# The S5 step-difference kernels: small matmuls ordered by product instead of by group, and a skip diagonal on 128 rows

## The chip, the cores and the metric

The kernel runs on one NeuronCore of a Trainium2 chip. The metric is the device time of one launch in microseconds (us), from the first to the last instruction with the little that lies around them; lower is better.

## The reference

The reference computes two layers of a bidirectional encoder on 512 tokens of 1024 channels, in float32. Layer 0 mixes tokens with a convolution and with retention; layer 1 mixes them with a bidirectional S5 state-space layer, and a GLU follows. Every layer ends with an MLP of 4096 hidden units. Shifts, scales and gates of the norms come from a conditioning vector.

Of the S5 layer this matters here: 64 groups of 16 channels each drive, in two directions, a diagonal complex state of 64 numbers, and the output is a sum of both directions and a skip:

```
bu = einsum('sgc,gpc->sgp', u, f * b)          # complex, per direction
h  = scan(h = a * h + bu)                      # forward, and backward
y  = Re(C_f h_f) + Re(C_b h_b) + d_skip * u
```

The kernel works in chunks of 8 tokens. Within a chunk the output at step i depends on the input at step j through a 16x16 matrix that depends on i - j alone, one for each step difference from -7 to 7. These matrices ("the kernel of the steps within a chunk") are products of C, powers of a and B, and at step difference 0 both directions and the diagonal of `d_skip` add up. They depend on the parameters only.

## The kernel before

The work is one program. Its stages, in order of time, are the mixer of layer 0 (to about 245 us), the MLP of layer 0 (to about 696 us), the S5 layer with its GLU, and the MLP of layer 1.

The large products run on TensorE (PE) in `mm3` (called from `gemm`, line 226): each operand is split in two halves in a reduced float32 type, and three matmuls of 128x128 weights by 512 columns add up in PSUM. All of them go through `mm`, line 170. A weight unit of 1024x128 takes 24 such matmuls. Each unit is loaded on SP's queue (`load_unit`, line 177), copied to its upper half on ScalarE (ACT, line 197), and its lower half is formed on VectorE (DVE, line 192), up to four units ahead.

While the MLP of layer 0 runs, a background generator prepares the S5 matrices in DRAM: first `s5_powers` (line 886), then `s5_matrices` (line 1116). `step` (line 147) takes pieces of it as units of the MLP go by, counted in estimated VectorE time (`pace`, 3.6 us a unit at line 1666). The order within an engine is then settled by the framework's scheduler, which simulates the program, except where an instruction is pinned in program order; the background's transfers (`put`, line 1121, on POOL's queue) are pinned, its matmuls are not.

`s5_matrices` works through 8 batches of 8 groups, each in 2 halves `s` of 4 groups: 16 blocks. For each block VectorE (lines 862 and 870) makes `e` (128 rows = direction and state; per group 2 x 128 columns, the real and the imaginary part) and `wi`, and from each batch `bp` (per group 32 columns: 16 of one direction, 16 of the other, zeros elsewhere; its zeros are set on POOL, line 1187). POOL's queue loads `pb`, `bt`, `bc` and `dk`, and stores `d_e`, `d_wi` and `d_kr`. Then come the matmuls that this text is about (lines 1240 to 1252). They fill one PSUM tile `ps`; group n writes the 32 partitions from 32n, that is, column group n of the array:

- two products (r = 0, 1) of `bp[r]` (32 columns as weights) and `e` (128 columns), line 1244;
- two products of the second half of `bp[r]` (16 columns) and the 16 columns of `e` at step difference 0, line 1249;
- the skip, line 1251: a 16x16 identity and `dk`, the diagonals of `d_skip` on 16 rows.

The loop over the four groups is the outer one, so all five products of a group stand together. Everything is plain float32, for which each product shows as two MATMUL records in the trace. At the end ScalarE copies `ps` to `kk` (line 1254), and POOL's queue stores it; `windows` (line 1153) later spreads it into the matrices that the S5 layer loads.

Another place of the kernel already addresses the four column groups in turn: `vecmat` (line 353), which multiplies a vector by weights for the modulation. Its weights are a broadcast column of `cT` or `mod` on 32 columns, and its inner loop runs over the column groups.

Of the kernel before, what the change touches and what calls it, by code (L numbers as in the profile page):

```python
# [10 lines left out]
F32 = mybir.dt.float32  # L11
# [6 lines left out]
P = 128  # L18
# [9 lines left out]
EPS = 1e-6  # L28
# blocks of adaLN that VectorE works out
# [3 lines left out]
# ---------------------------------------------------------------- host layout  # L33
def _units(w):
    """(K, M) weights -> [M/128][K/1024][128 (k in tile)][8 (k tile)][128 (m)]."""
    k, m = w.shape
    v = w.reshape(k // 1024, 8, P, m // P, P)
    return np.ascontiguousarray(v.transpose(3, 0, 2, 1, 4)).reshape(m // P, k // 1024, P, 1024)


def _consts():
# [12 lines left out]
    # row (16 g + c): [(any step, c)], [g]  # L54
# [10 lines left out]
def _layout(i):  # L65
# [6 lines left out]
    # [layer][256 columns][half of k][k in tile][k tile][column]  # L72
    o["adn"] = f["ada_w"].reshape(2, 2, 4, P, 24, 256).transpose(0, 4, 1, 3, 2, 5).reshape(2, 24, 2, P, 1024)
    # the same with columns first: [blocks of ADT][half][column][k]
# [21 lines left out]
    # [(direction, state)][batch of 8 groups][c_re, c_im, b_re, b_im][group][channel]  # L96
# [3 lines left out]
    # [4 groups][(step, channel)][re, im][(group, direction, state)]  # L100
    bt = np.stack([f["s5_" + n][0].transpose(3, 1, 0, 2).reshape(16, 16, 512) for n in ("b_re", "b_im")], axis=2)
    o["bt"] = np.tile(bt.transpose(1, 0, 2, 3), (1, 8, 1, 1))
    # the skip's weights on the diagonals of [batch of 8 groups][channel][group][channel]
# [13 lines left out]
class Stream:  # L117
    """Weight units in order, loaded and split ahead of their use."""
# [17 lines left out]
class Kern:  # L136
# [9 lines left out]
    # ------------------------------------------------------------ helpers  # L146
    def step(self, us):
        """Run background pieces worth about `us` of VectorE time."""
        self.debt += us * self.rate
        while self.debt > 0 and self.bg:  # L150
            try:
                c = next(self.bg[0])
                self.debt -= c
            except StopIteration:
                self.bg.pop(0)
        if not self.bg:
            self.debt = 0.0
# [17 lines left out]
    def load(self, out, src):  # L175
        """A load on SP's queue, whose order is the program's."""
        self.tc.keep_in_program_order(self.nc.sync.dma_start(out, src))
# [25 lines left out]
    def mm3(self, ps, w, k, x, first, last):  # L203
        """ps += w[k].T @ x with both operands in exact halves."""
# [5 lines left out]
    def gemm(self, src, count, xs, done, group=1, pace=0.0, onto=(), last=True):  # L210
        """For the next units of the stream: done(m, psum of unit.T @ xs); the
        units of a group go side by side, with the K tiles outermost. `pace` is
        the background work per unit; the first units add to what is in `onto`;
        without `last` the sums of the second half go on later."""
# [17 lines left out]
    def split(self, src, dst=None, tag=("hh", "hl")):  # L232
        """Exact halves of a float32 tile in SBUF."""
# [7 lines left out]
    # ------------------------------------------------------------ statistics  # L241
    def col_sums(self, ps, col, tiles):
        """ps[t, col + b] = sum over channels (partitions and tiles) of token b * 128 + t."""
# [5 lines left out]
    def rsqrt(self, ps, n, scale, two=False):  # L249
        """(scale * ps[:, :n] + EPS) ** -0.5; with `two`, ps[:, n:2n] counts as well."""  # L250
# [15 lines left out]
    def bcast(self, ps, v):  # L266
        """ps[:, token] = v (tokens on partitions, [128, 4])."""
# [3 lines left out]
    def add_sq(self, i, t, last=False):  # L271
        """Collect the sum of squares over the channel tiles."""
# [13 lines left out]
    def stats(self, early=lambda: None):  # L286
        """The tokens' 1 / rms, tokens on partitions; `early` is called when TensorE
        only waits for the last square."""
        # has the square root's table loaded early
# [7 lines left out]
    def rstd(self, *between):  # L297
        """The tokens' 1 / rms, on all partitions. `between`: functions to be called before
        each of TensorE's two steps, and after them; what ada_fill has loaded goes along."""
# [15 lines left out]
    def ada_ends(self):  # L315
        """Ends what the last rstd has taken along."""
        for d in self.ends:
            self.ada_end(*d)

    def norm_tiles(self, tiles, pb, gs, sh):  # L320
        """Halves of x * gs / rms + sh for these tiles; VectorE starts a tile before it
        ends the one before."""
# [19 lines left out]
    # ------------------------------------------------------------ adaLN  # L342
# [3 lines left out]
    def ada_mm(self, blk):  # L346
        """blk: layer, 256 columns and their weights, on TensorE with the K tiles in
        four column groups of the array."""
# [4 lines left out]
    def vecmat(self, v, w):  # L353
        """v.T @ 256 columns; w: for each part of them, its weights of K tile k."""
# [12 lines left out]
    def vecmat_end(self, ps, row):  # L367
        """Its 256 columns to partitions."""
# [25 lines left out]
    def ada_bg(self, l, ns):  # L394
        """Generator: loads a block, takes it in hand a step later."""
# [18 lines left out]
    def silu_c(self, tiles):  # L414
        """silu(c) on all partitions, for ada_dve"""
# [8 lines left out]
    def ada_dve(self, l, ns, raws=()):  # L424
        """Generator: these blocks, of ADT, on VectorE."""
# [16 lines left out]
    def ada_fill(self, l, n):  # L442
        """Two blocks, loaded now, for the next rstd to put between its steps."""
        self.fill = [(l, n + i, self.ada_load(l, n + i)) for i in range(2)]

    def ada_half(self, l, n):
        """A block's weights where the halves of hidden states were."""
# [11 lines left out]
    # ------------------------------------------------------------ layer 0 mixer  # L459
    def mixer0(self):  # L460
        nc, tc, a = self.nc, self.tc, self.a
        with ExitStack() as st:
# [9 lines left out]
            with tc.tile_pool(name="first", bufs=1) as first:  # L472
                # of each pair of channel tiles the shift on TensorE, the scale on VectorE
# [112 lines left out]
            # v, tokens on partitions  # L586
# [27 lines left out]
            # retention, with the gate's projection in between  # L614
# [33 lines left out]
            # conv LayerNorm, SiLU  # L648
# [41 lines left out]
            # the first units of the output's projection, as far as the convolution's part goes  # L690
# [53 lines left out]
    # ------------------------------------------------------------ MLP  # L744
    def pre(self, l, i):
        """Halves of x * g * (1 + scale), for the units that go ahead of the statistics."""
# [10 lines left out]
    def mlp(self, l, pace=0.0, each=lambda n: None):  # L757
        nc, a = self.nc, self.a
        # of the outputs, half stay in PSUM over the next quarter of the hidden units
# [7 lines left out]
        # the first units: rstd * (W.T @ xg) + W.T @ shift  # L767
# [77 lines left out]
    # ------------------------------------------------------------ S5: matrices  # L845
    def ops(self):
        """VectorE operations that add up their time, and a function that takes it."""
# [38 lines left out]
    def s5_powers(self, w1, w2, fr, fi, wo):  # L886
        """Generator: the powers of the S5 states. Like every background piece
        it yields its VectorE time."""
# [12 lines left out]
        with tc.tile_pool(name="pa", bufs=1, reuse_waits="tile") as pa:  # L901
# [14 lines left out]
            def exp(o, x):  # L916
                """o = exp(x); t1..t4 are scratch."""
# [13 lines left out]
                # 2^k as the product of two powers  # L931
# [18 lines left out]
            # ph modulo 2 pi, in two rounds; the parts of 2 pi have few bits  # L950
# [34 lines left out]
            # powers of a: pw[m] = a^m, m = 0..8  # L985
# [18 lines left out]
            # f = (a - 1) / lam  # L1004
# [16 lines left out]
            # unit phasors of 8 theta, kept at length one  # L1021
# [21 lines left out]
            # f' = f * conj(E)  # L1043
# [3 lines left out]
            # the angle of the other direction has the other sign  # L1047
# [20 lines left out]
            # per direction: powers for the inputs (8 - j | j + 1) and the outputs (i | 7 - i)  # L1068
# [16 lines left out]
            def turns():  # L1085
                for r in range(2):
# [7 lines left out]
                    # row = (16 groups, 8 steps) of part b -> [step][group][state]  # L1094
# [4 lines left out]
            # tables cos/sin(theta k), 8 groups a time  # L1099
# [16 lines left out]
    def s5_matrices(self, pl):  # L1116
        """Generator: the S5 matrices of every group, left in DRAM."""
# [14 lines left out]
        with tc.tile_pool(name="pb", bufs=1, reuse_waits="tile") as pb_:  # L1132
# [3 lines left out]
            def load(h):  # L1136
                """The operands of the inputs' matrices of 4 groups."""
# [8 lines left out]

            def load_bc(b):
                bc = tl("bc", [4, B, 16])
                dk = pb_.tile([16, B, 16], F32, name="dk", tag="dk", bufs=2)
                put(bc.rearrange("p r g c -> p r (g c)"), a["bc"][b])  # L1150
                put(dk.rearrange("p g c -> p (g c)"), a["dsk"][b])
                return bc, dk
            def windows(q):
                """The kernel of the steps within a chunk of 16 groups: moves for later."""
# [4 lines left out]
                def join():  # L1159
                    # [c'][group][step difference + 7][c]  # L1160
# [3 lines left out]
                def row(j):  # L1164
                    # row (j, c') holds the window that starts at step difference -j
# [11 lines left out]
            for b in range(G // B):  # L1177
# [3 lines left out]
                # f * b with the directions in separate columns  # L1181
# [12 lines left out]
                # their place is free now  # L1194
# [6 lines left out]
                for s in range(2):  # L1201
# [10 lines left out]
                    # three products: wr (cr + ci), ci (wr + wi), cr (wi - wr)  # L1212
# [27 lines left out]
                    for n in range(4):  # L1240
                        o = ps[32 * n:32 * n + 32, 0:P]
                        at = dict(tile_position=(0, 32 * n))
                        for r in range(2):
                            nc.tensor.matmul(o, lhsT=bp[r][:, s * 4 + n, :], rhs=e[:, n, r, :], start=r == 0,  # L1244
                                             stop=False, **at)
                        # step difference 0: both directions and the skip
                        o = ps[32 * n:32 * n + 16, 0:16]
                        for r in range(2):
                            nc.tensor.matmul(o, lhsT=bp[r][:, s * 4 + n, 16:32], rhs=e[:, n, r, 112:128], start=False,  # L1249
                                             stop=False, **at)  # L1250
                        nc.tensor.matmul(o, lhsT=self.ident[0:16, 0:16], rhs=dk[:, s * 4 + n, :], start=False,  # L1251
                                         stop=True, **at)
# [9 lines left out]
    # ------------------------------------------------------------ S5: the mixer  # L1262
# [435 lines left out]
```

## Time and profile before

| what | value |
|---|---|
| runs (3) | 1253.43, 1257.18, 1257.36 us |
| median | 1257.18 us |
| span of the profiled execution | 1255.3 us |
| PE busy | 1214.7 us (97% of the span) |
| VectorE busy | 875.9 us (70%) |
| ScalarE busy | 476.4 us (38%) |
| POOL busy | 109.0 us (9%) |

The profiled execution is given by its span, from the first to the last instruction; it lies 1.9 us below the median of the runs and within their spread. Engines are named PE (TensorE's matmuls), PEld (its weight loads, which overlap the matmuls), DVE (VectorE), ACT (ScalarE), POOL (GpSimd) and SP. A matmul's recorded duration is its way through the array; the next one can start long before it ends, so the pace of a row of matmuls is read from their starts. "x4" says that four like instructions follow each other in one row. A row of the view by stretches gives the stretch and its length, then for PE, PEld, DVE, ACT and POOL the busy time with the number of instructions, then the granted PE clock as a share of full speed (1.00 is 2.4 GHz), the mean busy share of the 16 DMA engines and the GB/s that they moved. A row of waits gives the total, the number of times and the longest, in us.

### The profile page before, as it was taken

The numbers are of one execution on the slowest core, as the hardware profiler recorded it, in microseconds if no ns is written. First come the engines' busy times: TensorE is split into PE (matmuls) and PEld (weight loads), VectorE is DVE, ScalarE is ACT, GpSimd is POOL, SyncE is SP. The second block draws the span as 40 slices with busy tenths as digits, with TensorE's granted clock in tenths as the row PEclk, the third lists the DMA queues.
The fourth block names the chain that finished last, engine by engine and source line by source line (L and its number), as shares of the span: only waits on it lengthen the run. The fifth ranks groups of instructions, "written<-read, shape, count | busy, mean of one in ns | idle before, by whom it ended". The sixth has DMA issues, their size and how long they took to land.

```text
span 1255.3 us, 17711 instructions
## 1 busy us (share of the span) xinstructions
PE 1214.7 (97%) x6830; PEld 967.1 (77%) x6830; DVE 875.9 (70%) x1605; ACT 476.4 (38%) x752; POOL 109.0 (9%) x221
## 2 busy tenths in 40 slices
PE   6999999999999999999999898999999999999996
PEld 4777756787788788888877777788888888888885
DVE  6899995898989778787767899869743332332333
ACT  4424314435514313312422657343552432532530
POOL 0000000000021222234332100000000000000000
PEclk6999999999999999999999889999999999999998
DMA  9754340724446787778697867648433332332201
GB/s 353 253 185 159 124 168 32 230 92 185 144 160 233 229 253 254 247 252 246 174 320 221 341 248 286 223 144 276 168 101 101 101 101 85 101 101 85 83 1 67
DMA packets 65700, 223.59 MB, mean 178 GB/s; under 512 B 11168, under 2 KB 11552, under 8 KB 63568
## 3 DMA queue, kind: packets, MB, share of 16 engines
q1 hardware_dynamic: 48528, 174.63, 41.0%
q0 software_dynamic: 16512, 46.79, 12.3%
q8 instruction: 53, 0.87, 0.3%
q10 hardware_dynamic: 576, 1.05, 0.2%
q14 instruction: 31, 0.25, 0.1%
HBM read 197.77 MB, written 29.82 MB: 181 GB/s over the span
## 4 chain that ended last, share of the span: by engine, by line
PE 89%; DVE 7%; DMA 2%; issue 1%; ACT 1%; SPq 0%; DVEq 0%; ACTq 0%
PE ps L170 84%; PE ps L1244 3%; DVE wk L1289 2%; DMA raw<-adn 1%; DVE xt L1421 1%; DVE xt L1420 1%; PE ps L1251 1%; PE ps L1249 0%; DMA raw<-fc 0%; DMA x<-x 0%; DVE wk L1677 0%; DVE sr L1289 0%; DVE hx L1289 0%; ACT wh L197 0%; SPq L1642 0%
## 5 line engine op out<-in xcount | busy, mean ns | idle before, releaser
L197 ACT CAST wh<-raw 128x1024 fp32r<-128x1024 f32 x169 | 176.7, 1050 | 514.3 <-PE ps L170 453.2
L192 DVE TENSOR_TENSOR wl<-raw,wh 128x1024 fp32r<-128x1024 f32 x169 | 205.8, 1221 | 194.1 <-ACT wh L197 191.9
L170 PE MATMUL ps<-hh,wh 128*128 128x512 f32 x808 | 317.6, 399 | 4.2 <-ACT cm L789 1.8
L170 PE MATMUL ps<-hl,wh 128*128 128x512 f32 x808 | 317.2, 393 | 1.6 <-DVE hl L238 1.1
L170 PE MATMUL ps<-hh,wl 128*128 128x512 f32 x808 | 316.5, 392 | 0.8 <-DVE wl L192 0.8
L170 PE MATMUL ps<-fh,wh 128*128 128x512 f32 x544 | 216.5, 399 | 0.0
L170 PE MATMUL ps<-fl,wh 128*128 128x512 f32 x544 | 215.6, 397 | 0.0
L170 PE MATMUL ps<-fh,wl 128*128 128x512 f32 x544 | 215.3, 396 | 0.0
L170 PEld LDWEIGHTS ps<-hh,wh 128*128 128x128 f32 x808 | 152.4, 189 | 42.9 <-ACT wh L197 3.5
L170 PEld LDWEIGHTS ps<-hl,wh 128*128 128x128 f32 x808 | 152.8, 189 | 33.8 <-DVE hl L238 1.6
L170 PEld LDWEIGHTS ps<-hh,wl 128*128 128x128 f32 x808 | 152.7, 189 | 33.9 <-DVE wl L192 1.2
L170 PEld LDWEIGHTS ps<-fh,wh 128*128 128x128 f32 x544 | 102.4, 188 | 25.5 <-issue 1.2
L170 PEld LDWEIGHTS ps<-fh,wl 128*128 128x128 f32 x544 | 102.5, 188 | 24.6
L170 PEld LDWEIGHTS ps<-fl,wh 128*128 128x128 f32 x544 | 102.5, 188 | 24.1
L827 DVE SCALAR_TENSOR_TENSOR x<-ps,mod,x 128x512 f32<-128x512 f32 x40 | 30.0, 750 | 77.9 <-PE ps L170 77.8
L538 DVE SCALAR_TENSOR_TENSOR cacc<-apad,cvw,cacc 128x512 f32<-128x512 f32 x120 | 83.5, 741 | 0.0
L811 DVE TENSOR_TENSOR fl<-wk,fh 128x512 fp32r<-128x512 f32 x64 | 44.1, 689 | 21.5 <-ACT fh L810 21.5
L280 ACT ACTIVATE wk<-x 128x512 f32<-128x512 f32 x35 | 22.1, 631 | 52.5 <-DVE x L827 27.1
L862 DVE TENSOR_TENSOR w<-pb,bt 128x512 f32<-128x512 f32 x64 | 41.3, 686 | 0.6
L436 DVE SCALAR_TENSOR_TENSOR raw<-raw,x 128x512 f32<-128x512 f32 x52 | 33.2, 686 | 11.8 <-DMA raw<-adt 9.4
L807 ACT ACTIVATE wk<-wk 128x512 f32<-128x512 f32 x64 | 40.7, 635 | 1.5
L1244 PE MATMUL ps<-eb,bp 128*32 128x128 f32 x256 | 40.9, 279 | 0.0
(246 smaller groups left out, 1373.0 us busy)
## 6 DMA issues: line engine op xcount, KB each, us to landing
raw<-fc SPq DMA_DIRECT2D x128, 512.0 KB, 4.0
raw<-adn SPq DMA_DIRECT2D x50, 512.0 KB, 5.2
raw<-adt SPq DMA_DIRECT2D x34, 512.0 KB, 4.6
pb<-d_pw POOLq DMA_DIRECT2D x32, 256.0 KB, 8.0
bt<-bt POOLq DMA_DIRECT2D x16, 512.0 KB, 8.8
d_e<-eb POOLq DMA_DIRECT2D x16, 512.0 KB, 3.5
d_wi<-eb POOLq DMA_DIRECT2D x16, 512.0 KB, 7.3
wi<-d_wi SPq DMA_DIRECT2D x8, 1024.0 KB, 5.4
```

Of the source, the lines that this page charges most:

```text
L170: i = self.nc.tensor.matmul(out, lhsT=lhsT, rhs=rhs, start=start, stop=stop, **kw)
L192: self.keep(self.nc.vector.tensor_tensor(lo, raw, hi.bitcast(F32), SUB))
L197: self.keep(self.nc.scalar.copy(hi, raw))
L280: nc.scalar.activation(sq, t, AF.Square)
L436: self.keep(nc.vector.scalar_tensor_tensor(half, half, 1.0, self.cb[k], MUL, MUL, accum_out=v[:, 2 * k + h:2 * k + h + 1]))
L538: nc.vector.scalar_tensor_tensor(ac, ap[:, t:t + S], cvw[:, i * TAPS + t:i * TAPS + t + 1], ac, MUL, ADD)
L807: nc.scalar.activation(f, r, AF.Square)
L811: nc.vector.tensor_tensor(lo, f, hi.bitcast(F32), SUB)
L827: nc.vector.scalar_tensor_tensor(self.x[m], ps, gate[:, m:m + 1], self.x[m], MUL, ADD)
L862: V.tensor_tensor(o, x, y, op)
L1244: nc.tensor.matmul(o, lhsT=bp[r][:, s * 4 + n, :], rhs=e[:, n, r, :], start=r == 0, stop=False, **at)
L1289: pin(nc.vector.tensor_tensor(*args))
```

## The change

The loop over products becomes the outer one, and the loop over the four groups the inner one, in a small function `each`. The skip's operands get all 128 rows: the identity's first 16 columns are used on all its rows, and `dk` becomes two fixed tiles of 128 rows that POOL sets to zero once, of which the transfers fill rows 0 to 15. Comments are taken out elsewhere in the file, which shifts line numbers and no instructions.

```diff
+            dks = []
+            for n in range(2):
+                dk = pb_.tile([P, B, 16], F32, name=f"dk{n}")
+                nc.gpsimd.memset(dk, 0.0)
+                dks.append(dk)
+
             def load_bc(b):
                 bc = tl("bc", [4, B, 16])
-                dk = pb_.tile([16, B, 16], F32, name="dk", tag="dk", bufs=2)
+                dk = dks[b % 2]
                 put(bc.rearrange("p r g c -> p r (g c)"), a["bc"][b])
-                put(dk.rearrange("p g c -> p (g c)"), a["dsk"][b])
+                put(dk[0:16].rearrange("p g c -> p (g c)"), a["dsk"][b])
                 return bc, dk
...
                     ps = self.psum()
-                    for n in range(4):
-                        o = ps[32 * n:32 * n + 32, 0:P]
-                        at = dict(tile_position=(0, 32 * n))
-                        for r in range(2):
-                            nc.tensor.matmul(o, lhsT=bp[r][:, s * 4 + n, :], rhs=e[:, n, r, :], start=r == 0,
-                                             stop=False, **at)
-                        o = ps[32 * n:32 * n + 16, 0:16]
-                        for r in range(2):
-                            nc.tensor.matmul(o, lhsT=bp[r][:, s * 4 + n, 16:32], rhs=e[:, n, r, 112:128], start=False,
-                                             stop=False, **at)
-                        nc.tensor.matmul(o, lhsT=self.ident[0:16, 0:16], rhs=dk[:, s * 4 + n, :], start=False,
-                                         stop=True, **at)
+                    def each(rows, cols, ops, start=False, stop=False):
+                        for n in range(4):
+                            lhs, rhs = ops(n)
+                            nc.tensor.matmul(ps[32 * n:32 * n + rows, 0:cols], lhsT=lhs, rhs=rhs, start=start,
+                                             stop=stop, tile_position=(0, 32 * n))
+                    for r in range(2):
+                        each(32, P, lambda n: (bp[r][:, s * 4 + n, :], e[:, n, r, :]), start=r == 0)
+
+                    for r in range(2):
+                        each(16, 16, lambda n: (bp[r][:, s * 4 + n, 16:32], e[:, n, r, 112:128]))
+                    each(16, 16, lambda n: (self.ident[:, 0:16], dk[:, s * 4 + n, :]), stop=True)
```

## Rows read from the trace of the kernel before

**Rows 1.** The chain that ended last: its shares by line, and one piece.

```profile
PE ps L170 84%; PE ps L1244 3%; DVE wk L1289 2%; DMA raw<-adn 1%; DVE xt L1421 1%; DVE xt L1420 1%; PE ps L1251 1%; PE ps L1249 0%; DMA raw<-fc 0%; DMA x<-x 0%; DVE wk L1677 0%; DVE sr L1289 0%; DVE hx L1289 0%; ACT wh L197 0%; SPq L1642 0%
...
473.23 11.12 PE ps L170 x48
```

**Rows 2.** The view by stretches, over the 16 blocks.

```profile
430.00:690.00 260.00, 260.00 (x1528) 209.37 (x1527) 202.04 (x357) 73.26 (x108) 81.45 (x149) 1.00 0.79 244
```

**Rows 3.** PE's timeline around one block: start, length (us), instructions.

```profile
601.70 0.39 PE L170 MATMUL ps<-hh,wl 128*128 128x512 f32 x1
602.02 0.62 PE L1244 MATMUL ps<-eb,bp 128*32 128x128 f32 x4
602.48 0.26 PE L1249 MATMUL ps<-eb,bp 128*16 128x16 f32 x4
602.66 0.21 PE L1251 MATMUL ps<-dk,ident 16*16 16x16 f32 x2
...
605.16 0.50 PE L170 MATMUL ps<-hh,wh 128*128 128x512 f32 x1
605.49 0.39 PE L170 MATMUL ps<-hl,wh 128*128 128x512 f32 x1
```

**Rows 4.** The shapes: duration in ns (min, median, max), first and last start.

```profile
L1244 PE MATMUL ps<-eb,bp x256: 272/273/298, 434.9 to 687.5; 128*32 128x128 f32 x128
...
L1249 PE MATMUL ps<-eb,bp x256: 175/176/180, 437.3 to 687.7; 128*16 128x16 f32 x128
```

**Rows 5.** PE's timeline where a block is split in two.

```profile
630.22 0.39 PE L170 MATMUL ps<-hh,wl 128*128 128x512 f32 x1
630.54 0.41 PE L1244 MATMUL ps<-eb,bp 128*32 128x128 f32 x2
...
631.21 0.39 PE L170 MATMUL ps<-hl,wh 128*128 128x512 f32 x1
...
632.37 0.40 PE L170 MATMUL ps<-hh,wh 128*128 128x512 f32 x1
...
635.95 0.39 PE L170 MATMUL ps<-hh,wl 128*128 128x512 f32 x1
```

**Rows 6.** PE's timeline over one row of `vecmat`, then its first 0.09 us.

```profile
285.11 1.06 PE L170 MATMUL ps<-raw,mod 128*32 128x128 f32 x32
286.10 0.61 PE L170 MATMUL ps<-sel,adr 128*128 128x1 f32 x4
...
285.11 0.29 PE L170 MATMUL ps<-raw,mod 128*32 128x128 f32 x4
```

**Rows 7.** POOL: its memset; `pb`'s first load issued, and its first use.

```profile
L1187 POOL MEMSET bp<- x16: 307/312/389, 413.5 to 650.1; 128x256 f32 x16
...
410.70 1.26 POOL L1122 DMA_DIRECT2D pb<-d_pw  x2
...
432.96 1.28 DVE L862 TENSOR_TENSOR w<-pb,bt 128x512 f32<-128x512 f32 x2
```

**Rows 8.** The view by stretches: an earlier one, the first four blocks, one piece.

```profile
310.00:400.00 90.00, 90.00 (x421) 72.12 (x420) 80.50 (x187) 36.48 (x52) 10.75 (x20) 1.00 0.52 173
...
430.00:490.00 60.00, 60.00 (x361) 48.33 (x360) 48.29 (x91) 13.11 (x19) 16.89 (x32) 1.00 0.82 250
...
640.00:650.00 10.00, 10.00 (x68) 7.27 (x67) 5.62 (x8) 2.42 (x5) 1.15 (x3) 1.00 1.05 338
```

**Rows 9.** Who waited for whom, 430 to 690 us: total, times, longest.

```profile
DVE wl L192 <- ACT wh L197: 18.6, 16, 2.9
DVE raw L436 <- DMA raw<-adt: 7.9, 3, 2.8
DVE wk L1270 <- DMA wk<-k_chan: 5.9, 1, 5.9
DVE bp L862 <- POOL bp L1187: 4.6, 4, 1.3
PEld ps L1244 <- DVE w L862: 1.5, 4, 0.4
```

## The prediction

> **What bounds the kernel now.** I read three views in turn. The chain that ended last comes first: 84% of it is the large matmuls of line 170, and the three lines of the small matmuls, 1244, 1249 and 1251, stand in it too [rows 1]. Next, the view by stretches from 430 to 690 us, which holds all 16 blocks: PE is busy for 260.00 of 260.00 us at full clock, DVE for 202.04, POOL for 81.45, and the DMA engines for a share of 0.79 [rows 2]. So here, and this is the only place where the change acts, PE sets the time, and what PE is spared comes off the end as long as nothing else fills the gap. Last, PE's timeline shows what a block costs, by starts, since durations overlap.
>
> A large matmul takes 0.232 us (48 in 11.12 us [rows 1]). Around an unbroken block the large matmuls at 601.70 and 605.49 lie 3.79 us apart; two such steps would be 0.46, so the block costs 3.33 [rows 3]. Of this, 3.14 are four groups of 0.785 each (602.02 to 605.16), and 0.19 is the way in and out: the first small matmul starts 0.32 after the large one, not 0.23, and the second large one 0.33 after the first.
>
> Within a group, the four matmuls of 128 columns take 0.46 (602.02 to 602.48). The four of 16 columns last 0.176 each and 0.26 together, so their starts are (0.26 - 0.176) / 3 = 0.028 apart, and the skip starts 0.18 after the first of them: 0.10 of that is a pause. The next group starts 0.145 after the first of the two skip records (602.02 + 0.785 - 602.66), and one step of some 0.04 (0.21 together, less a length as of line 1249) between the two leaves again 0.10 as a pause [rows 3, 4]. The skip is the one product on 16 rows, and PE pauses before and after it.
>
> In 4 of the 16 blocks the scheduler has put the first product apart, with large matmuls between: 630.22 to 631.21 is 0.99, less 0.46 makes 0.53, and 632.37 to 635.95 is 3.58, less 0.46 makes 3.12; together 3.65 [rows 5]. One block is in four parts; with 0.32 for each further part (3.65 - 3.33) I put it at 3.33 + 3 x 0.32 = 4.3. All blocks: 11 x 3.33 + 4 x 3.65 + 4.3 = **55.5 us**.
>
> **The change, part by part.**
>
> *Products in turn over the column groups.* The nearest row is `vecmat`, which has the same shape (128 rows, 32 columns of weights, 128 moving columns, float32) and already goes over the four groups: 32 matmuls, eight rounds of four, take 0.99 us up to the next instruction (285.11 to 286.10). The first four alone end 0.29 after the first start, and one of this shape lasts 0.273 [rows 4], so they start within 0.02 of each other [rows 6]. Even with the last one's way out counted in, a round takes no more than 0.99 / 8 = 0.124, about what one matmul takes in its group now (0.46 / 4 = 0.115). The 16 matmuls of 128 columns in a block are four rounds of 0.115: 0.46 in place of 1.84.
>
> *The 16-column products and the skip.* The skip gets the row count, the columns and the shape of line 1249, so I price it as that. A block has 16 + 8 = 24 such matmuls in six rounds. No row shows this shape in turn over groups, so I bound it. Low: a round takes what one matmul takes in one group, 0.028, as it did for 128 columns; 6 x 0.028 = 0.17. High: each record needs 0.028 whatever its group, 24 x 0.028 = 0.67. I take the low end, since the burst of rows 6 has four starts within 0.02, under one such step; both ends stay for the range. The Trainium skill speaks for the high end: "TensorEngine Tiling (Array Packing)", section Instruction Overhead, says that each matmul carries an overhead of about 60 cycles and warns against tiling a dimension that is already small. By that rule 24 records of 25 ns (an estimate from that page: 60 cycles at 2.4 GHz) would take 0.60, and the burst in rows 6 disagrees with it only over four records.
>
> *The two pauses per group go*, eight of 0.10 in a block, since all products now have 128 rows; one exit of 0.10 stays at the block's end.
>
> A block then costs 0.19 + 0.46 + 0.17 + 0.10 = **0.92** (high end 1.42). If the same five blocks are split once, five times 0.32 is added. All blocks: 16 x 0.92 + 1.6 = 16.3, so PE is spared 55.5 - 16.3 = **39.2 us** (high end: 16 x 1.42 + 1.6 = 24.3, spared 31.2).
>
> *POOL.* Two memsets of 128x128 come ahead of the first loads; one of 128x256 takes 0.31 [rows 7], so at most 0.62 in all. `pb` is issued at 410.70 and first used at 432.96, so 22 us cover it: nothing. Without that cover the first block would be 0.62 later. The transfers into `dk` keep their number, bytes and place in POOL's queue. The fixed pair is reused every second batch, as the two buffers before: nothing. The weights of the skip have the columns of line 1249's. ScalarE's copy to `kk`, and POOL's memset of `bp` behind it, are only released earlier.
>
> *What is late next.* DVE keeps its 202.04 us, and the stretch shrinks to 260 - 39.2 = 220.8: DVE would be 91% busy. From 310 to 400 us it is 80.50 / 90 = 89% busy beside a PE without a gap [rows 8], so this is near what the kernel already bears. The waits of DVE for neither PE nor the casts (which themselves wait for PE) are 7.9 + 5.9 + 4.6 = 18.4 [rows 9]; 202.0 + 18.4 = 220.4 just fits into 220.8. In the first 60 us, with four blocks, it doesn't: 48.29 [rows 8] and their part of the waits by time, 18.4 x 60 / 260 = 4.2, are 52.5, where PE would need 60 - 4 x 2.45 = 50.2 (39.2 / 16 = 2.45). That is 2.3 us over, and PE's own waits for DVE at a block's start, 1.5 now [rows 9], will grow. I allow 3 us given back in all, between 0 and the 18.6 that DVE waits for casts [rows 9] if those waits should stay. The DMA share rises from 0.79 to 0.79 x 260 / 221 = 0.93; pieces at 1.05 run beside a full PE now [rows 8], so I cost it at nothing, with rival C if that fails.
>
> **Sum.** 39.2 - 3 = 36.2 us less. The working is in the time of one execution, whose span of 1255.3 us lies 1.9 under the median of the runs, within their spread; taken off the median, 1257.2 - 36.2 = **1221.0 us**.
>
> **The rivals.**
> A. *Forecast*, 1221.
> B. *Small records do not overlap*, the high end above: spared 31.2, and with DVE less pressed some 1 given back: 1227. For it: nothing shows a lasting pace under 0.028 a record. Against: the burst.
> C. *DVE or the transfers become the bound.* If DVE's 18.6 us of waits for casts stay beside the rest, the stretch cannot go below 220.4 + 18.6 = 239: spared 21, 1236. For it: DVE's stretches at 91%, and a DMA share of 0.93. Against: those casts wait for PE to free buffers, and PE will free them sooner; and rows 8.
> D. *The products do not overlap, only the pauses go* (the scheduler, which is free to order these matmuls, might also undo the turn): a block keeps 16 x 0.115 + 24 x 0.028 = 2.51 of its 3.14, so 0.63 x 16 = 10 us spared, 1247. Against: rows 6, the same shape in turn.
> E. *Slower: a change of column group pauses PE as a change to 16 rows does.* A block has 39 changes; at 0.10 each that is 3.9 on top of 2.51, 6.4 in place of 3.14, 16 x 3.3 = 52 us more, 1309. It decides from (3.14 - 2.51) / 39 = 0.016 us a change. Against: rows 6 change the group at every matmul, and 32 of them take 0.99 in all.
>
> **How the numbers follow.** Chances: A 0.49, B 0.20, C 0.20, D 0.06, E 0.03, and 0.02 for no effect by something unseen. The low end of the range is A with nothing given back and no split, 1257.2 - 39.2 - 1.6 = 1216, and 1 to 2 for the spread of runs: 1215. The high end takes in B and most of C: 1235. About 0.3% (4 us) is what a measurement of this kernel can tell from no change; A to D lie beyond it on the fast side: faster 0.95, same 0.02, slower 0.03.
>
> **What would show it.** In the changed kernel, PE's timeline around a block should have 16 matmuls of the first shape in one row with 0.46 to the next, 24 of the second within 0.2 (A) or 0.6 (B), no pause between 1249's and the skip's successors, and about 1.4 us between the large matmuls on both sides. PE should stay near 100% busy from 430 to about 651 us, DVE near 91%. Gaps on PE that end with DVE or a transfer in that stretch mean C; starts 0.11 apart within one round mean D; 0.2 apart mean E. The S5 layer and the last MLP should keep their lengths; if they don't, a step of this working is wrong.

## The result and the profile after

The changed kernel takes **1225.39 us** (median of 4 runs, 1224.28 to 1227.6) beside 1256.49 for the kernel before (4 runs, 1253.43 to 1257.36): a ratio of 0.9752, 95% interval 0.9736 to 0.9769, or 31.1 us less. The forecast was 36.2 less. The profiled execution of the changed kernel took 1225.63 us. Line numbers of the changed kernel lie some 7 higher; all small matmuls now have line 1252.

The page of the changed kernel, its span and two engines:

```profile
span 1223.9 us, 17714 instructions
...
PE 1175.5 (96%) x6830; PEld 932.9 (76%) x6830; DVE 873.4 (71%) x1605; ACT 475.9 (39%) x752; POOL 109.4 (9%) x223
```

PE's busy time is 39.2 us less than before, and the span 31.4: the other 7.8 are idle time of PE that was not there, most of it in the stretch of the 16 blocks, as the rows below show. VectorE does nearly the same work as before (873.4 and 875.9 us). The first matmul of the S5 layer behind the stretch (`hl,wi`) starts at 671.39 and did so at 703.19 before. That is 31.8 earlier; from there to the end it takes 552.5 and took 552.1. So the whole effect arises ahead of the S5 layer, in the stretch of the 16 blocks, as forecast.

PE's timeline around an unbroken block (start, length, instructions), beside [rows 3]:

```profile
590.00 0.39 PE L170 MATMUL ps<-hh,wl 128*128 128x512 f32 x1
590.32 0.74 PE L1252 MATMUL ps<-eb,bp 128*32 128x128 f32 x32
590.88 0.22 PE L1252 MATMUL ps<-dk,ident 128*16 128x16 f32 x8
591.04 0.50 PE L170 MATMUL ps<-hh,wh 128*128 128x512 f32 x1
591.37 0.39 PE L170 MATMUL ps<-hl,wh 128*128 128x512 f32 x1
```

From the large matmul at 590.00 to the second one behind the block at 591.37 are 1.37, less two steps of 0.23: a block costs **0.90**, where it cost 3.33. The x32 holds the 16 records of 128 columns and 16 of 16 columns; those of the skip follow at 590.88. The first to the last of the 40 starts takes 0.609, of which the wide products are 0.46 and the 24 small ones 0.15. The last pause, from the last start to the next large matmul, is 0.106.

The view by stretches (length, then PE, PEld, DVE, ACT, POOL, granted clock, DMA share, GB/s), beside [rows 2, 8]:

```profile
430.00:490.00 60.00, 60.00 (x405) 48.26 (x404) 56.38 (x110) 17.65 (x26) 18.38 (x35) 1.00 0.90 287
490.00:560.00 70.00, 69.23 (x478) 54.74 (x477) 60.65 (x107) 20.72 (x30) 27.70 (x51) 1.00 0.89 274
...
600.00:630.00 30.00, 29.41 (x196) 22.64 (x195) 18.64 (x33) 7.72 (x12) 9.94 (x18) 1.00 0.91 294
630.00:640.00 10.00, 6.06 (x59) 4.53 (x58) 9.92 (x18) 4.06 (x5) 1.84 (x4) 0.91 0.88 326
640.00:650.00 10.00, 10.00 (x42) 8.06 (x41) 9.97 (x16) 2.76 (x6) 3.35 (x6) 0.92 0.97 258
...
430.00:661.00 231.00, 225.70 (x1540) 179.10 (x1539) 201.77 (x360) 74.71 (x110) 80.83 (x148) 0.99 0.88 274
```

PE is no longer full: 231.00 - 225.70 = 5.30 us of gaps, most of them from 630 to 640. There the granted clock falls as well: 0.91 and 0.92 in the two pieces of 10 us are 0.9 + 0.8 = 1.7 us lost, that is 3.4 us at 1.2 GHz. From 600 to 630 VectorE is busy for 18.64 of 30 only, and from 630 to 650 it is full: it stood still first and then had to catch up. The waits (total, times, longest) of VectorE, PE and ScalarE in the stretch, beside [rows 9], say for what:

```profile
DVE wk L1277 <- DMA wk<-k_chan: 9.1, 1, 9.1
DVE raw L436 <- DMA raw<-adt: 5.9, 2, 4.0
DVE wl L192 <- ACT wh L197: 3.5, 5, 1.2
...
PE ps L1252 <- DVE eb L862: 2.4, 1, 2.4
PE ps L1252 <- DVE eb L870: 1.5, 1, 1.5
...
ACT wh L197 <- DMA raw<-fc: 10.2, 2, 10.0
```

The wait for `k_chan` rose from 5.9 to 9.1, and ScalarE waited 10.0 for a weight unit (`raw<-fc`). The waits of VectorE for casts went from 18.6 to 3.5, those for POOL's `bp` are gone. `k_chan` is a table of 68 KB that `by_group` (line 1268), another piece of the background, needs for shift and scale of the S5 layer; VectorE's order is fixed, so while it waits for the table the next `eb` isn't made. SP's queue (issue, length, transfers) shows what stood ahead of that load:

```profile
573.87 0.33 SPq L177 DMA_DIRECT2D raw<-fc  x1
603.49 6.85 SPq L177 DMA_DIRECT2D hh<-adn  x8
610.98 0.33 SPq L177 DMA_DIRECT2D wk<-k_chan  x1
615.41 5.24 SPq L177 DMA_DIRECT2D raw<-fc  x4
623.55 8.04 SPq L177 DMA_DIRECT2D raw<-adn  x4
```

Nothing is issued for 29 us; the queue's own waits put that down to the large matmuls (29.3 at a time, 38.2 before), which must free buffers first. Then come eight transfers of 256 KB, two modulation blocks (`ada_half`, line 447) that the program loads at the start of the last quarter of the MLP (line 832) into buffers which must first come free; behind them stand the table, four weight units and four halves of further modulation blocks, all within 28 us. The table's 68 KB landed 17.1 us after their issue (11.9 before), the weight units 13.1 after theirs (12.2 before). PE's gaps over 1 us follow (the bracket holds the gap and what ended it):

```profile
636.08 0.43 PE L1252 MATMUL ps<-eb,bp 128*32 128x128 f32 x8 [2.44 <-DVE eb L862]
638.01 0.54 PE L1252 MATMUL ps<-eb,bp 128*32 128x128 f32 x17 [1.50 <-DVE eb L870]
```

### The profile page after: what moved, and what is told of

It is laid out like the page before. It is cut to its first block, busy times and chain, and to the rows that moved or that the text cites. A ratio compares the mean times of both kernels' runs of the same rounds, so it can differ in the third digit from the quotient of the medians.

```text
span 1223.9 us, 17714 instructions
## 1 busy us (share of the span) xinstructions
PE 1175.5 (96%) x6830; PEld 932.9 (76%) x6830; DVE 873.4 (71%) x1605; ACT 475.9 (39%) x752; POOL 109.4 (9%) x223
## 4 chain that ended last, share of the span: by engine, by line
PE 83%; DVE 8%; DMA 5%; ACT 2%; issue 1%; SPq 0%; DVEq 0%; ACTq 0%
PE ps L170 83%; DVE wk L1296 2%; DMA wk<-k_chan 1%; DMA raw<-adn 1%; DVE xt L1428 1%; DMA raw<-adt 1%; DVE xt L1427 1%; PE ps L1252 1%; DVE wl L192 0%; DMA raw<-fc 0%; DMA x<-x 0%; DVE hx L1296 0%; DVE wk L1684 0%; ACT wh L197 0%; DVE sr L1296 0%
## 5 line engine op out<-in xcount | busy, mean ns | idle before, releaser
L170 PEld LDWEIGHTS ps<-fh,wl 128*128 128x128 f32 x544 | 102.7, 189 | 24.8
L810 ACT CAST fh<-wk 128x512 fp32r<-128x512 f32 x64 | 39.8, 622 | 1.7
```

The costliest lines, as they stand in the source:

```text
L170: i = self.nc.tensor.matmul(out, lhsT=lhsT, rhs=rhs, start=start, stop=stop, **kw)
L810: nc.scalar.copy(hi, f)
```

## The experiments

Theory 1, after this reading: the blocks cost what was forecast, and the missing 4 to 5 us are VectorE's wait for `k_chan`. Rivals: VectorE's amount of work, which would fill the shortened stretch in any case (theory 2 in the expectations), and the whole burst on SP's queue, whatever waits for it (theory 3). Beside these, three kernels take the change apart. Each ratio is against the kernel before on the same chip (medians 1256.17, 1256.61, 1258.13 and 1256.92 us for the four sets of runs).

### The changed kernel once more

No edit.

> The changed kernel once more, on the chip of the next three runs, so that they can be compared with it: some 31 us under the kernel before, ratio 0.975. Its profile tells whether the gap of PE near 630 us, behind VectorE's wait of 9.1 us for the table k_chan, comes again: theory 1 (one late transfer costs it) expects a wait of 5 to 10 us in the same place; theory 2 (VectorE is full all along) expects gaps of PE in changing places.

1224.47 us, ratio 0.9753 (0.9734 to 0.9773). `k_chan` is waited for 9.0 us in the same place, PE's gaps are 231.00 - 226.01 = 4.99: the pattern repeats.

### Only the skip on 128 rows, groups outermost

```diff
-                    for r in range(2):
-                        each(32, P, ...)
+                    for n in range(4):
...
-                        nc.tensor.matmul(o, lhsT=self.ident[0:16, 0:16], rhs=dk[:, s * 4 + n, :], ...)
+                        nc.tensor.matmul(o, lhsT=self.ident[:, 0:16], rhs=dk[:, s * 4 + n, :], ...)
```

> Only the second half of the change: the skip's operands on 128 rows, the loop over the groups outermost as before. Theory: the two pauses of 0.10 at each group go, and nothing overlaps, so a block falls from 3.04 between first and last start to some 2.4, and the kernel is 10 us faster than before, 1247. Rival: the pauses belong to the change of column group and not to the 16 rows, so the block and the time stay as before.

1242.93 us, ratio 0.9895 (0.9878 to 0.9911): 13.2 less. PE's timeline of a block:

```profile
604.10 0.62 PE L1253 MATMUL ps<-eb,bp 128*32 128x128 f32 x4
604.56 0.23 PE L1258 MATMUL ps<-eb,bp 128*16 128x16 f32 x3
604.62 0.30 PE L1253 MATMUL ps<-eb,bp 128*32 128x128 f32 x1
604.64 0.18 PE L1258 MATMUL ps<-eb,bp 128*16 128x16 f32 x1
604.67 0.20 PE L1260 MATMUL ps<-dk,ident 128*16 128x16 f32 x2
604.76 0.49 PE L1253 MATMUL ps<-eb,bp 128*32 128x128 f32 x3
```

The pauses around the skip are gone. A group takes 0.52 (604.10 to 604.62) in place of 0.785, more than the 0.20 of the two pauses, because the next group's first matmul starts amid the small ones of this group. First to last start is 2.15 in this block; with way in and out it costs 2.45, so 16 x (3.33 - 2.45) = 14.1 is what PE is spared. PE has no gap in the stretch (231.00 of 231.00) and nearly all of it shows. It also gives a check on the loss in the changed kernel: from here to there PE is spared 16 x (2.45 - 0.90) = 24.8 more, and 7.0 go to gaps and clock (5.3 + 1.7), leaving 17.8; measured are 1242.93 - 1224.47 = 18.5.

### Only the turn, the skip on 16 rows

```diff
-                dk = dks[b % 2]
+                dk = pb_.tile([16, B, 16], F32, name="dk", tag="dk", bufs=2)
...
-                    each(16, 16, lambda n: (self.ident[:, 0:16], dk[:, s * 4 + n, :]), stop=True)
+                    each(16, 16, lambda n: (self.ident[0:16, 0:16], dk[:, s * 4 + n, :]), stop=True)
```

> Only the first half of the change: products in turn over the column groups, the skip left on 16 rows. Theory: PE pauses 0.10 before and after the eight skip records, once in a block, so a block takes 0.2 longer than in the changed kernel; 16 blocks make 3 us, 1228 if PE is the bound. If VectorE is the bound of the stretch (theory 2), PE's 3 us are hidden and the time is the changed kernel's, 1225.

1225.31 us, ratio 0.9753 (0.9729 to 0.9778). The block here:

```profile
583.11 0.39 PE L170 MATMUL ps<-hh,wl 128*128 128x512 f32 x1
583.43 0.74 PE L1243 MATMUL ps<-eb,bp 128*32 128x128 f32 x32
584.10 0.23 PE L1243 MATMUL ps<-dk,ident 16*16 16x16 f32 x8
584.25 0.50 PE L170 MATMUL ps<-hh,wh 128*128 128x512 f32 x1
```

From the first small matmul to the next large one are 0.82 in place of 0.72: one pause of 0.10 ahead of the skips, the one behind them being there in any case. This is the place to weigh a rule: the Trainium skill, "TensorEngine Tiling (Array Packing)", section Tiling Modes, says that a change of the tiling mode, not of the tile, drains the array. The rows agree and give the size, a pause of 0.10 at a change to or from 16 rows, and none at a change of column group. The expectation had 0.2 for a block; 0.10 in 16 blocks make 1.6 us, which the time can't show, with an interval of some 3 us to either side. So once the products take turns, the 128 rows of the skip are worth 1.6 us of PE's time, and of the kernel's time an amount that these runs can't tell from nothing.

### The wide products in turn, the small ones by group

```diff
-                    for r in range(2):
-                        each(16, 16, lambda n: (bp[r][:, s * 4 + n, 16:32], e[:, n, r, 112:128]))
-                    each(16, 16, lambda n: (self.ident[:, 0:16], dk[:, s * 4 + n, :]), stop=True)
+                    for n in range(4):
...
```

> The changed kernel with only the products of 128 columns in turn; the products of 16 columns and the skip go group by group again, on 128 rows. Six matmuls of one group then follow each other, four times; if each takes the 0.026 to 0.028 that they took in the kernel before, a block has 24 x 0.027 = 0.65 in place of 0.15 behind its first 0.46, 0.5 more; 16 blocks make 8 us more for PE. Theory of a PE-bound stretch: 1232. If the waits behind the blocks are what sets the stretch, most of it is hidden: 1226 to 1229.

1226.42 us, ratio 0.976 (0.9743 to 0.9777). First to last start of a block is 0.80 here, of which the 24 small ones take 0.34 in place of 0.15; 0.65 was expected, so the small ones of different groups overlap in part even in this order. So PE loses 16 x 0.19 = 3.0, of which its smaller gaps (231.00 - 227.13 = 3.87 in place of 5.30) give 1.4 back; the 1 to 2 us that are left are within the interval. That the changed kernel passes part of this saving on to gaps would fit, but the times don't show it.

### The table four units earlier

`by_group` stops once behind its load, and the background starts it in the last quarter of the MLP:

```diff
                 fs.append((hi, lo))
+                if q == 3 and m == 4 and l == 0:
+                    next(bg)
...
         self.load(chan[:, 0:136], self.a["k_chan"])
+        yield
```

> The changed kernel with the load of k_chan issued four weight units earlier, so that VectorE need not wait for it. Theory 1, that the 9.1 us wait for this table is what gave back most of the 7 us between what the blocks spare (39) and what the run gained (31 to 32): PE's gaps of 3.9 and 0.6 us and the half clock behind them (1.7 us) go, so 5 to 6 us faster than the changed kernel, some 1220, and PE without a gap from 430 to 660. Theory 2, that VectorE's 202 us of work is the bound of the shortened stretch anyway: the gaps move elsewhere, less than 2 us faster than the changed kernel.

1228.23 us, ratio 0.9784 (0.9763 to 0.9806): 3.8 slower than the changed kernel in the same set of runs. The waits of this kernel from 605 to 645 us:

```profile
DVE wl L192 <- ACT wh L197: 11.0, 3, 10.1
ACT wh L197 <- DMA raw<-fc: 10.3, 2, 10.0
...
PE ps L1254 <- DVE eb L864: 5.8, 1, 5.8
```

The wait for `k_chan` is gone. VectorE now waits as long for a cast, which waits for a weight unit behind the same eight transfers; PE's gap grows to 5.8 in one piece, all gaps in the stretch to 231.00 - 223.58 = 7.42, and the clock is at 1.2 GHz for 6.8 us after it. 7.4 + 3.4 is 3.8 more than the 7.0 of the changed kernel. **Theory 1 falls**: the table was what VectorE met first, not what was scarce.

### The two modulation blocks later

```diff
-                if q == 3 and n == 0 and l == 0:
-                    self.fill2 = [self.ada_half(1, m) for m in (8, 9)]
+                if q == 3 and n in (4, 6) and l == 0:
+                    self.fill2 = getattr(self, "fill2", []) + [self.ada_half(1, 6 + n // 2)]
```

> The changed kernel, with the two modulation blocks (8 loads of 256 KB, hh<-adn) that SP issues in the last quarter of the MLP ahead of its last four weight units issued four and six units later, behind them. Theory 3, that the gap of PE near 630 us comes from the transfers: those 2 MB go ahead of the last weights, whose casts then wait 10 us for them, and k_chan is caught in the same jam. Then the waits for raw<-fc and k_chan shrink to some 3 us, PE's gaps of 4.5 us and the half clock behind them go, and the kernel takes some 1219, 5 to 6 under the changed kernel. Theory 2, VectorE as the bound: VectorE's busy share stays where it was, the gap moves, less than 2 us.

1223.79 us, ratio 0.9739 (0.9719 to 0.9759). Gaps of 3.95, none over 1.7, and the clock stays at 2.4 GHz throughout the stretch; by these 3.0 us should be won. Behind the stretch 1.2 of them are lost again: PE's gaps from the end of the stretch to the S5 layer's first large matmul are 2.5 here and 1.4 in the changed kernel. The ratio shows 1.8, within the interval, so by its time this run settles nothing.

### Both edits together

> As the run before, and k_chan loaded four units earlier besides. Theory 3: the early load of k_chan cost nothing by itself and is of little use once the jam is gone: the same time as with the blocks later alone, within 2 us, some 1218 to 1220. Theory 1 (k_chan itself): this one is faster than the run before by 4 us or more.

1220.85 us, ratio 0.972 (0.9705 to 0.9734). The stretch of this kernel, and its largest waits on VectorE:

```profile
430.00:661.00 231.00, 229.05 (x1567) 181.42 (x1565) 203.04 (x364) 74.84 (x111) 81.57 (x149) 1.00 0.88 277
```

```profile
DVE raw L436 <- DMA raw<-adt: 8.9, 3, 4.9
DVE x L829 <- PE ps L170: 5.8, 6, 3.0
```

`k_chan` lands 7.8 us after its issue and VectorE doesn't wait for it. Gaps are 1.95 (0.87 and 1.08, at 517 and 523 us), the clock doesn't fall in the stretch; DVE's work and the DMA share are those of the changed kernel (203.04 and 0.88). So it is when the loads on SP's queue are issued, not the amount of VectorE's work or of the transfers, that cost the 5 us (7.0 less 1.95), of which the time shows about 4. The rest is lost again at the entry to the S5 layer, where PE waits for VectorE longer than in the changed kernel (first row: both edits; second: the changed kernel; 1.4 before, too):

```profile
PE ps L1344 <- DVE wk L1299: 2.7, 2, 2.3
PE ps L1341 <- DVE wk L1296: 1.4, 2, 1.0
```

### Control: the kernel before, with the blocks later

The edit of the blocks alone, on the kernel before.

> The kernel before, with the same two blocks loaded later. Before the change PE had no gap in this stretch although the same transfers stood ahead of the last weights, so every theory expects no change here: 1256, within 2 us. If it is faster by 4 us or more, then the later loads help for a reason of their own, behind the stretch, and the run of the changed kernel with them proves nothing about its gap.

1257.39 us (10 runs), ratio 1.0009 (0.9999 to 1.0019). In the kernel before the place of these loads costs nothing that the time shows.

### Control: the kernel before, with both edits

Both edits, on the kernel before.

> The kernel before with both edits (the two modulation blocks later, the table four units earlier): the control to the pair on the changed kernel. If the burst on SP's queue costs time only because the blocks got shorter, PE has no gap from 430 to 690 us here, as before, and the time is that of the kernel before, 1256 to 1258 us, ratio 0.998 to 1.002. If the two edits are an improvement of their own, whatever the blocks take, some 4 us go here too: about 1253, ratio 0.997.

1257.67 us (12 runs), ratio 1.0003 (0.9992 to 1.0014). The stretch of [rows 2] in this kernel:

```profile
430.00:690.00 260.00, 259.93 (x1502) 208.94 (x1501) 202.18 (x359) 74.93 (x109) 79.92 (x146) 1.00 0.78 243
```

PE has 0.07 us of gaps, next to none without the edits [rows 2], and the 4 us that they give the changed kernel are outside this interval. At the entry to the S5 layer PE waits 2.7 here as well, so the edits cost the same there. Only with the shorter blocks did the order in SP's queue matter.

### Both edits, measured again on another chip

> The changed kernel with both loads moved (the two blocks later, k_chan earlier) once more, on the chip of the next two: some 1221, 4 us under the changed kernel, ratio 0.972, with PE's gaps in the stretch near 2 us, all of them at 516 to 523 us.

1222.43 us, ratio 0.9726 (0.9703 to 0.975); gaps of 0.87 and 1.08 in the same two places. Two measurements agree: 3.3 to 4.1 us under the changed kernel by the ratios.

### Both edits, and one block's products a step later behind their loads

```diff
-            yield from (self.ada_dve if n in dve else self.ada_bg)(l, [n])
+            g = (self.ada_dve if n in dve else self.ada_bg)(l, [n])
+            yield next(g)
+            if n == 7:
+                yield 0.0
+            yield from g
```

> As the run before; of the last modulation block that VectorE works out in the stretch, the products come one step of the generator (three weight units) later behind its loads, so that VectorE does not wait for raw<-adt (4.9 and 1.8 us near 505 and 513). Theory 3 (late transfers cause every gap that is left): the two gaps at 516 to 523, 2 us, go, 1219. Theory 2 (VectorE has too much work there): they stay or move, 1221.

1222.16 us, ratio 0.9716 (0.9696 to 0.9737): not to be told from the kernel with both edits. Gaps of 1.26 and 1.08 stay, and so does the wait for `raw<-adt` (9.3 in all). The edit met another load than the one waited for; a miss.

### Both edits, and two blocks of the modulation from VectorE to TensorE

```diff
-                ada = self.ada_either(1, list(range(8)), [3,4,5,6,7])
+                ada = self.ada_either(1, list(range(8)), [5,6,7])
```

> As the first run of these three, with two of the five modulation blocks that VectorE works out in the MLP of layer 0 (blocks 3 and 4) given to TensorE: VectorE loses some 6 us of work, TensorE gains two rows of 16 small matmuls, some 1.3 us each with the way in and out. Theory 2 (VectorE as the bound): gaps shrink, 1219. Theory 3: PE is the bound again in that part, and pays: 1221 to 1224.

1227.11 us, ratio 0.9762 (0.9743 to 0.9781): 4.7 slower than with both edits alone in the same set. The same stretch:

```profile
430.00:661.00 231.00, 225.60 (x1551) 177.86 (x1550) 197.21 (x352) 74.01 (x109) 79.09 (x145) 0.99 0.88 279
```

VectorE has 6 us less work than with both edits alone, and PE more gaps, 5.40. The two longest, 1.39 and 2.98, end at 518 and 522 us, where both edits alone have 0.87 and 1.08, and the clock is at 1.2 GHz for 3.4 us behind them. So less work for VectorE doesn't by itself fill PE. That its work isn't what limits the rest is not settled by this, since TensorE's blocks bring loads and products of their own.

## Why the prediction was right, and where it was off

**The block** was right in every term. Way in and out as given; four wide rounds of 0.46; the small products at the low end (0.17 forecast, 0.15 measured); one exit of 0.10: 0.92 forecast, 0.90 measured. Four blocks are still split, three in two and one in three (a fifth has PE's waits inside it): by the starts all blocks are 16 x 0.905 + 3 x 0.35 + 0.9 = 16.4, forecast 16.3. The 39.2 that PE is spared stands.

**Rival B is out by the timeline, not by the time.** Its 1227 is nearer to 1225.39 than the forecast's 1221, so the time alone would have spoken for it; but its cause, 24 records one after the other in 0.67, isn't there: they take 0.15. The rule weighed in that place (the Trainium skill, "TensorEngine Tiling (Array Packing)", Instruction Overhead) gave 0.60 by an estimate from that page; the trace disagrees, with 0.15, for records that take turns over the four groups. D is out too: the four starts of a round lie within 0.02, not 0.11 apart. E is out: a change of group costs no pause; only the change to 16 rows does, as the run with the turn alone shows.

**The term that was mis-sized is "I allow 3 us given back in all".** Given back were 5.3 of gaps and 1.7 at the lower clock, 7.0: 39.2 - 7.0 = 32.2, and the S5 layer starts 31.8 earlier. Two steps behind that term failed.

First, its place. The allowance was worked out for the first 60 us, where VectorE was to be 2.3 over. There PE has no gap at all (60.00 of 60.00, VectorE 56.38). The forecast that the waits for casts would go held (18.6 to 3.5), and that for `bp` went as well; that they went because PE frees buffers sooner isn't shown by any run.

Second, "I cost it at nothing", of the DMA share. The mean share rose to 0.88 (0.93 forecast), and a high share in a piece indeed ran beside a full PE, before as after. But the price wasn't in the share, it was in the order of one queue: with each block shorter by 2.4 us there was less PE work in hand to cover the burst with the eight modulation transfers at its head, and the wait for the table, which before cost PE nothing at 5.9 us, at 9.1 us stood between PE and its next block. By the prediction's own sign, gaps of PE that end with VectorE, that is rival C's mechanism, in its transfer form, at 4 to 5 of its 15 us. Shown: both loads moved give most of it back, and the same two moves change nothing that the time of the kernel before shows; the table's alone makes it worse, and the blocks' alone can't be told from nothing. That the shorter blocks leave less PE work in hand shows in the two traces. In both kernels SP issues the first of the eight loads behind the same large matmul, the 2164th in either trace (at 631.86 before, at 603.49 after), and 116 more stand between that and the 15th block. The stretch of the first 112 of them, with the small matmuls between, before (first row) and after (second), and the start of the 15th block before:

```profile
631.86:665.18 33.32, 33.32 (x191) 26.09 (x191) 23.54 (x42) 9.53 (x15) 9.40 (x18) 1.00 1.00 342
603.49:632.53 29.04, 28.45 (x185) 22.35 (x185) 17.67 (x35) 7.31 (x12) 7.90 (x15) 1.00 0.99 326
...
666.22 0.63 PE L1244 MATMUL ps<-eb,bp 128*32 128x128 f32 x4
```

PE has 28.45 us of work where it had 33.32, 4.9 less, beside a DMA share of 0.99 and 1.00. Before, it came to the 15th block 34.4 us after the issue, and what the block needs was there. Now the block could start 32.6 us after the issue (636.08), and PE had run out 2.44 us sooner; with the gap of 0.59 ahead of it and the 1.50 within the block, 4.5 us of gaps stand against the 4.9 of work that are gone. Also in this term was no allowance for the clock, which fell after PE's gaps.

Left open: the 2 us of gaps around 517 to 523 us, a few us behind a wait of VectorE for `raw<-adt`; that this wait is their cause isn't shown. They stand in both measurements with both edits, and one attempt missed them. Of all kernels run, the change with both edits is the fastest that was measured twice, 1220.85 and 1222.43 us.

## What to carry to other kernels

Small matmuls that use a quarter of the array's columns overlapped nearly fully here once consecutive ones went to different column groups, so the order of the loops decides: from a block's first small matmul to the next large one, the order alone made 0.82 us of 3.14, and the skip on 128 rows 0.72 of that. When an engine that set the time is spared a lot, look for the in-order queue whose bursts that engine's work had covered, and read its issue times, not its mean share. A wait named by the profile may only be the first in line behind the burst: taking that one away made the kernel slower, and moving the burst as well made it faster.

## What was not expected of the hardware

- Records of 16 columns that take turns over the groups need 0.149 us for 24, that is 6 ns each, where in one group they start 25 to 29 ns apart.
- With the skip on 128 rows, a group's first wide matmul started 0.06 after the first small one of the group before and ahead of its last three, so that a group took 0.52, less than its parts one after the other (0.46 and six small ones of some 0.026, 0.62).
- The length of a gap alone didn't decide whether the clock fell to 1.2 GHz behind it. In the stretch it was at 1.2 GHz for 3.4 us behind gaps of 2.44 and 1.50 in the changed kernel, for 3.4 behind 0.79 and 1.50 with the turn alone, and for 6.8 behind 5.80 with the early table. A gap of 2.17 at 521 us with the turn alone and, with the blocks later, gaps of 1.20, 1.09 and 1.66 were followed by no fall.
